# Own raw buffers for two weights of the output projection, and another order of temporaries in the first FFN product

## The chip, the cores and the metric

One core of a Trainium2 chip runs the whole program; the other cores are idle. The metric is the device time of one execution in microseconds (us), taken as the median of several runs. A profiled execution stands beside it, with a trace of every instruction. The engines are named as the profile names them: PE (matrix products, with PEld for its weight loads), DVE (vector engine), ACT (scalar engine), POOL (GpSimd) and SP (which here only issues transfers).

## The reference, cut to what matters

A decoder layer on 1024 tokens of width 1024: two attention branches are merged by gates, projected and added to the input; then a norm, a SwiGLU feed-forward net with inner width 2816, a second residual and a last norm.

```python
merged = (g_a * y_a + g_b * y_b).astype(x.dtype)
x = x + merged @ w_out[layer]                      # output projection

h2 = rms_norm(x, norm_ffn_g[layer])
gu = h2 @ w_ffn_in[layer]                          # first FFN product
x = x + (jax.nn.silu(gu[..., :D_FF]) * gu[..., D_FF:]) @ w_ffn_down[layer]
return rms_norm(x, norm_final_g)
```

Everything is float32.

## The kernel before, in words

**Splitting.** A float32 factor is split into a high part (a rounded copy by ACT, line 99) and a low part (the rest, by DVE, line 100); `split` does both. A product is then three matmuls: high by high, high by low, low by high (`mm3`, lines 104 to 106; `prod`, line 306). `load_w` asks for a raw weight on SP's queue (line 123), into a raw buffer with the tag `wr` (two buffers in `wpool`, unless it is given another pool as `rpool`), and splits it. A raw buffer is free again when DVE has made the low part. The parts lie in `w` tiles (two buffers in `wpool`) or, for tag `wo`, in two buffers of the stage's own pool. In the profile all raw buffers are named wr, all high parts wh and all low parts wl, after the names that the program gives its tiles.

**Output projection.** The stage runs twice over halves of 512 output columns (`c0` = 0 and 512), within each over two halves of 512 tokens (`hh`), within these over four groups `t` of 128 tokens; each group has a bank of PSUM and 24 matmuls, eight `k` of three. A weight tile covers two `k`, so each column half has four, `ws[0]` to `ws[3]`: the first two with their parts in `wpool`, the last two (k = 4 and 6) under `wo` in the stage's pool `mpool`. All four raw weights go through `wpool`'s two raw buffers. `pd()` hands out the banks from six in turn. `take(t)` adds a finished bank to the residual `x1` on DVE (line 1025). In the second column half the row of 128 tokens is then complete: `take` writes it out and calls `norm_transpose`, which squares it on ACT into a tile `hn` (line 174), works out the norm's factor on DVE, writes the normed row into `hn` (line 176), transposes it on PE in two groups of four (line 181) into a bank from a ring of two, splits the transposed values into `hT` and keeps an unsplit copy (line 187). `hn` has four buffers.

**Right sides.** Beside this, `right_side(n)` loads two blocks of the second FFN weight on SP (line 997), subtracts quarters from each other on POOL (line 1001) and writes the results out (line 1002), for eight `n`, with three buffers `r`; `sides(a, b)` does so for a range. They are used only in the last stage.

**First FFN product.** The first two of 22 column blocks are plain products (`plain(0)`, `plain(1)`, pool "first": a pad of 12 KB per partition and two buffers `a` of 4 KB). `plain(0)` starts with the first token half, placed around the last transposes (`behind`), and ends with the second. The others run as a block scheme of seven products instead of eight (`up`, pool "up"): `left_side` makes A1, S12, S34 and A22 out of raw weights, the sums on POOL (tile `s`), the parts by `split`; `c1`, `v2`, `v3`, `sg1` hold intermediate results and `a` the output. A1 is multiplied first, then S12. Pool "up" lies where pool "first" lay, so each of its tiles waits for what was in its place.

**Who orders the work.** Each engine takes its instructions strictly in a written order. That order is made at build time by a planner with cost estimates of its own; `tc.issue_after(i)` puts the instructions of a block behind `i` on the engine of `i`. `reserve` only claims places, in the order of its list, which fixes where each tile of the pool lies. The pool of the last stage, "down", lies in turn over hT, the block scheme's tiles and pool "up".

Of the kernel before, what the change touches and what calls it, by code (L numbers as in the profile page):

```python
# [8 lines left out]
F32 = mybir.dt.float32  # L9
F32R = mybir.dt.float32r  # L10
# [5 lines left out]
P = 128  # L16
D = 1024
S = 1024
KT = D // P
NT = S // P  # L20
HALF = 512
# [26 lines left out]
def layer_kernel(  # L48
# [59 lines left out]
    last_mm, last_hi, last_lo, last_sq = [None], [None], [None], [None]  # L108
# [104 lines left out]
    hT = [hT_all[:, :, hh * HALF:(hh + 1) * HALF] for hh in range(2)]  # L213
# [59 lines left out]
    def reserve(pool, *places):  # L273
        for tag, shape, dtype, bufs in places:
            for _ in range(bufs):
                pool.tile([P] + shape, dtype, tag=tag, name=nm(tag), bufs=bufs)
# [128 lines left out]
    with pool_of("foxv", 2) as vpool:  # L405
# [49 lines left out]
        for i in range(NT):  # L455
            load_x()
            hh, c = divmod(i * P, HALF)
# [115 lines left out]
    with pool_of("proj", 1) as upool:  # L573
# [3 lines left out]
        for pr in range(0, 4, 2):  # L577
            for a in range(2):
                c0 = FOX0 + a * FOX_W + pr * P
# [23 lines left out]
    fpool = f_ctx.__enter__()  # L603
# [305 lines left out]
    for i, (br, dt) in enumerate(merge_order):  # L909
        n = br * KT + dt  # L910
# [58 lines left out]
    TWO_ROWS = [(j, j + 1) for j in range(2, NFF - 4, 2)]  # L969
# [15 lines left out]
    blocks = [(f1[:], f3[:]), (f2, f4)]  # L985
# [4 lines left out]
    with pool_of("wout", 2) as mpool:  # L990
        gain2 = load_gain(mpool, norm_ffn_g)

        def right_side(n):

            r = mpool.tile([P, 2, 2, HALF], F32, tag="r", name=nm("r"), bufs=3)
            j = TWO_ROWS[n][0]
            last_w[0] = nc.sync.dma_start(out=r[:].rearrange("p n b c -> p n (b c)"),
                              in_=w_ffn_down[j * P:(j + 2) * P, :].rearrange("(n p) c -> p n c", p=P))
            b11, b12, b21, b22 = [r[:, i, b] for i in range(2) for b in range(2)]
            for out, p, q in ((b11, b12, b11), (b12, b22, b12), (b22, b22, b11), (b21, b22, b21)):  # L1000
                nc.gpsimd.tensor_tensor(out=out, in0=p, in1=q, op=ALU.subtract)
            nc.gpsimd.dma_start(out=rows_of(right_dram[n]), in_=r[:].rearrange("p n b c -> p (n b) c"))

        def sides(a, b):
            for n in range(a, b):
                with tc.issue_after(last_w[0].ins):
                    right_side(n)

        for c0 in range(0, D, HALF):
            ws = []  # L1010

            def load_out(k):
                src = w_out[k * P:(k + 2) * P, c0:c0 + HALF]
                ws.append(load_w(src, 2, HALF) if k < 4 else load_w(src, 2, HALF, tag="wo", pool=mpool))

            for hh in range(2):
                pts = [pd() for _ in range(4)]

                def mms(t, k):
                    mm3(pts[t][:], hT[hh][:, k, t * P:(t + 1) * P], ws[k // 2][:, k % 2], k == 0, k == KT - 1)  # L1020

                def take(t):
                    xt = x1[2 * hh + t // 2][:, t % 2]
                    xs = xt[:, c0:c0 + HALF]
                    nc.vector.tensor_tensor(out=xs, in0=pts[t][:], in1=xs, op=ALU.add)
                    if c0 > 0:
                        nc.scalar.dma_start(out=x1_dram[4 * hh + t], in_=xt)
                        norm_transpose(xt, gain2, hT[hh], t * P, mpool, True, 4, blocks[hh])

                if hh == 0 and c0 == 0:  # L1030
                    for k in range(KT):
                        if k % 2 == 0:
                            load_out(k)
                            if k < 6:
                                with tc.issue_after(last_w[0].ins):
                                    x_rows(k // 2)
                        for t in range(4):
                            mms(t, k)
                    sides(0, 3)
                    with tc.issue_after(last_w[0].ins):  # L1040
                        x_rows(3)
                    for t in range(4):
                        take(t)
                    continue
                if hh == 0:
                    for k in range(0, KT, 2):
                        load_out(k)
                        if k == 2:
                            sides(3, 5)
                    sides(5, len(TWO_ROWS))  # L1050
                for t in range(4):
                    for k in range(KT):
                        with tc.issue_after(last_mm[0].ins) if k == 0 else ExitStack():
                            mms(t, k)
                    take(t)


    a_dram = dpool.tile([NFF, P, S], F32, name="a_dram")
# [13 lines left out]
    with pool_of("first", 2) as fpool:  # L1072
# [48 lines left out]
        rpool = r_ctx.__enter__()  # L1121
# [1 line left out]
        split(T1.hi, T1.lo, f1[:])  # L1123

    with pool_of("up", 1) as fpool:
        reserve(fpool, ("s", [KT, P], F32, 2), *[("s34" + n, [KT, P], F32R, 1) for n in "hl"],
                *[("a22" + n, [4, P], F32R, 1) for n in "hl"],
                *[(n, [HALF], F32, 1) for n in ("c1", "v2", "v3", "sg1")], ("a", [S], F32, 2))

        def tmp(n):  # L1130
            return fpool.tile([P, HALF], F32, tag=n, name=nm(n), bufs=1)

        def up(j, todo, half):
            A1, S12, S34, A22 = left_side(fpool, *(odd if j == PLAIN + 1 else raws(j)), 2, 1)
            b1, b2, b3 = pd(), pd(), psf.tile([P, HALF], F32, tag="f", name=nm("pf"))
            a = fpool.tile([P, S], F32, tag="a", name=nm("a"), bufs=2)
            a1, a2 = a[:, :HALF], a[:, HALF:]
            c1, v2, v3, sg1 = [tmp(n) for n in ("c1", "v2", "v3", "sg1")]
            prod(b1, A1[:, :4], B11, True)
            with tc.issue_after(s12_hi[0].ins) if j == PLAIN else ExitStack():  # L1140
                nc.scalar.activation(out=c1[:], in_=b1[:], func=AF.Copy)
            prod(b2, S12[:, 4:], T2, True)
            vi = from_bank(v2[:], b2, c1)
            if todo:
                with tc.issue_after(vi.ins):
                    left_rows(*todo, 1)
            prod(b1, A1[:, 4:], B21)

            nc.scalar.activation(out=sg1[:], in_=b1[:], func=AF.Sigmoid)
            gi = from_bank(sg1[:], b1, sg1, ALU.mult)  # L1150
            if todo:
                with tc.issue_after(gi.ins):
                    left_rows(*todo, 2)
            prod(b2, S34[:, :4], T3)
            from_bank(v3[:], b2, c1)
            prod(b3, S12[:, :4], T1, True)
            ai = from_bank(a2, b3, v3)
            if half:
                with tc.issue_after(ai.ins):
                    left_rows(None, half, None, 0)  # L1160
            prod(b2, A22, T4)
            from_bank(a1, b2, c1)
            nc.gpsimd.tensor_tensor(out=a1, in0=a1, in1=sg1[:], op=ALU.mult)
            prod(b3, S34[:, 4:], B22)
            gt2, sg2 = tmp("v3"), tmp("sg1")
            from_bank(gt2[:], b3, v2)
            nc.scalar.activation(out=sg2[:], in_=gt2[:], func=AF.Sigmoid)
            nc.gpsimd.tensor_tensor(out=sg2[:], in0=gt2[:], in1=sg2[:], op=ALU.mult)
            nc.gpsimd.tensor_tensor(out=a2, in0=a2, in1=sg2[:], op=ALU.mult)
            return a[:].rearrange("p (b c) -> p b c", b=2)  # L1170

        def left_rows(n, p, q, part):

            if part == 0:
                ops = [(2, p[:, 0], p[:, 1], ALU.subtract)]
            elif part == 1:
                ops = [(0, p[:, 1], q[:, 1], ALU.add)]
            else:
                ops = [(1, f1[:, 0], p[:, 0], ALU.subtract), (3, q[:, 0], f1[:, 1], ALU.subtract)]
            for i, x_, y_, op in ops:  # L1180
                nc.vector.tensor_tensor(out=f1[:, i], in0=x_, in1=y_, op=op)
            if part == 2:
                nc.gpsimd.dma_start(out=rows_of(left_dram[n, 3:7]), in_=f1[:])

        todo, one = None, None
        for j in range(PLAIN, NFF):
            n, second = divmod(j - 2, 2)
            a = up(j, todo, one if second and n < len(TWO_ROWS) else None)
            todo = None
            if n >= len(TWO_ROWS):  # L1190
                nc.gpsimd.dma_start(out=a_dram[j], in_=a.rearrange("p b c -> p (b c)"))
            elif second:
                nc.gpsimd.dma_start(out=rows_of(left_dram[n, 1:3]), in_=a)
                todo = (n, one, a)
            else:
                nc.gpsimd.dma_start(out=left_dram[n, 0], in_=a[:, 0])
                one = a
# [187 lines left out]
```

## Time and profile before

| | |
|---|---|
| median of 3 runs | 1468.31 us (1468.17 to 1468.74) |
| the profiled execution | 1467.87 us |
| its span, first to last instruction | 1466.2 us |
| PE busy | 1439.0 us, 98% of the span |
| DVE, ACT, POOL busy | 945.9, 562.7, 493.0 us |
| mean granted clock of PE | 0.992 |

In the trace the first column half of the output projection ends at about 750.7 us, the second at about 806 us, the two plain products at about 853 us; the block scheme then runs to about 1243 us and the last stage to the end. How to read it: a row of a timeline gives start, duration, engine, line, operation, the tile written, the tiles read, the shapes and a count; in brackets stands how long the engine had been idle before, and what ended that. A row of waits gives the total, the number of waits and the longest. "ACTq" or "SPq" is an engine's queue of transfers to issue. PEclk is the clock that PE was granted, 1.00 at full speed. A busy PE is not a PE at full speed.

### The profile page before, as it was taken

What the parts mean: (1) busy time and instruction counts of PE and PEld (TensorE: products, weight loads), DVE (VectorE), ACT (ScalarE), POOL (GpSimd) and SP (SyncE); (2) the same over time, 40 slices, a digit from 0 to 9 for tenths busy, and PEclk for the clock granted to TensorE, in tenths of its full rate; (3) what the DMA queues carried; (4) which work ended last, traced back from release to release, by engine and by line L of the source; (5) the groups of instructions that cost most, each with busy time, mean ns of one, the idle gap of its engine ahead of it and who ended that gap; (6) DMA issues with size and microseconds to landing.
All of it is one profiled execution on the core that took longest, in us unless ns stands there. A gap on an engine that the chain in (4) does not pass through costs nothing.

```text
span 1466.2 us, 18397 instructions
## 1 busy us (share of the span) xinstructions
PE 1439.0 (98%) x6876; PEld 1165.2 (79%) x6876; DVE 945.9 (65%) x1332; ACT 562.7 (38%) x840; POOL 493.0 (34%) x438
## 2 busy tenths in 40 slices
PE   8999999999999999999989999999999999999997
PEld 7898888877777676788868878888888888888886
DVE  6484554359888999846626854566655655765655
ACT  5333332226656423354315522223322223644333
POOL 1021444535433321110074035566666664100000
PEclk9999999999999999999999999999999999999999
DMA  8232444575543561265796322233332332976512
GB/s 231 72 101 80 150 158 129 141 204 134 129 123 98 173 201 36 80 233 172 263 333 258 93 75 64 95 108 108 108 102 99 108 115 101 350 253 230 182 48 86
DMA packets 165785, 213.58 MB, mean 146 GB/s; under 512 B 13760, under 2 KB 115136, under 8 KB 165440
## 3 DMA queue, kind: packets, MB, share of 16 engines
q1 hardware_dynamic: 129376, 119.06, 25.8%
q0 software_dynamic: 15344, 55.59, 10.6%
q10 hardware_dynamic: 20976, 37.76, 8.2%
q8 instruction: 54, 0.88, 0.3%
q14 instruction: 35, 0.29, 0.1%
HBM read 146.32 MB, written 66.06 MB: 145 GB/s over the span
## 4 chain that ended last, share of the span: by engine, by line
PE 89%; DVE 6%; issue 1%; DMA 1%; ACT 1%; POOL 1%; SPq 1%; ACTq 0%; POOLq 0%; DVEq 0%
PE pd L306 30%; PE pd L1300 10%; PE pf L306 7%; PE pd L105 6%; PE pd L106 6%; PE pd L104 6%; PE pf L106 3%; PE pf L105 3%; PE pf L104 3%; PE pd L203 2%; PE pd L204 2%; PE pd L207 2%; PE pd L718 1%; PE pd L667 1%; PE pd L668 1%
## 5 line engine op out<-in xcount | busy, mean ns | idle before, releaser
L306 PE MATMUL pd<-tT,wh 128*128 128x512 f32 x768 | 235.5, 390 | 2.8 <-ACT wh L99 2.8
L100 DVE TENSOR_TENSOR wl<-wr,wh 128x1024 fp32r<-128x1024 f32 (+2 forms) x110 | 129.6, 1178 | 136.1 <-ACT wh L99 135.3
L99 ACT ACTIVATE wh<-wr 128x1024 fp32r<-128x1024 f32 (+2 forms) x110 | 95.4, 867 | 289.9 <-PE pd L306 163.0
L306 PEld LDWEIGHTS pd<-tT,wh 128*128 128x128 f32 x768 | 144.2, 188 | 33.2 <-ACT wh L99 3.2
L306 PE MATMUL pd<-hT_t,wh 128*128 128x512 f32 x536 | 167.0, 392 | 0.0
L306 PE MATMUL pd<-tT,wl 128*128 128x512 f32 x384 | 147.6, 389 | 0.0
L306 PEld LDWEIGHTS pd<-hT_t,wh 128*128 128x128 f32 x536 | 101.7, 190 | 21.6 <-ACT cc L332 0.2
L106 PE MATMUL pf<-hT_t,wl 128*128 128x512 f32 x288 | 114.1, 397 | 0.0
L104 PE MATMUL pf<-hT_t,wh 128*128 128x512 f32 x288 | 113.6, 395 | 0.0
L105 PE MATMUL pf<-hT_t,wh 128*128 128x512 f32 x288 | 113.2, 393 | 0.0
L292 POOL TENSOR_TENSOR s<-wr 128x512 f32<-128x512 f32 x29 | 53.3, 1839 | 157.9 <-DMA wr<-in_w_in_dram 72.9
L99 ACT ACTIVATE wh<-s 128x1024 fp32r<-128x1024 f32 x58 | 61.4, 1060 | 114.4 <-POOL s L293 87.3
L306 PE MATMUL pd<-hT_t,wl 128*128 128x512 f32 x268 | 105.0, 392 | 0.0
L99 ACT ACTIVATE oh<-raw 128x1024 fp32r<-128x1024 f32 x66 | 70.0, 1062 | 81.0 <-PE pd L1300 28.9
L306 PE MATMUL pf<-hT_t,wh 128*128 128x512 f32 x320 | 99.1, 391 | 0.0
L100 DVE TENSOR_TENSOR wl<-s,wh 128x1024 fp32r<-128x1024 f32 x58 | 71.7, 1238 | 33.9 <-ACT wh L99 33.9
L1300 PE MATMUL pd<-ol,oh 128*128 128x512 f32 x224 | 87.1, 389 | 0.0
L1300 PE MATMUL pd<-oh,ol 128*128 128x512 f32 x224 | 86.3, 389 | 0.0
L1300 PE MATMUL pd<-oh 128*128 128x512 f32 x224 | 84.7, 389 | 0.0
L104 PE MATMUL pd<-wh,hT_t 128*128 128x512 f32 (+1 forms) x208 | 77.7, 383 | 6.8 <-ACT wh L99 6.6
L306 PEld LDWEIGHTS pd<-tT,wl 128*128 128x128 f32 x384 | 72.1, 188 | 14.9
L105 PE MATMUL pd<-wl,hT_t 128*128 128x512 f32 (+1 forms) x208 | 80.0, 385 | 1.9 <-DVE wl L100 1.9
(287 smaller groups left out, 3234.1 us busy)
## 6 DMA issues: line engine op xcount, KB each, us to landing
wr<-in_w_in_dram SPq DMA_DIRECT2D x46, 512.0 KB, 4.6
wr<-in_w_ffn_in_dram SPq DMA_DIRECT2D x44, 512.0 KB, 3.8
raw<-left_dram SPq DMA_DIRECT2D x56, 256.0 KB, 5.3
g_dram<-fst ACTq DMA_DIRECT2D x32, 256.0 KB, 2.3
land<-g_dram SPq DMA_DIRECT2D x16, 512.0 KB, 3.5
r<-in_w_ffn_down_dram SPq DMA_DIRECT2D x8, 1024.0 KB, 8.5
right_dram<-r POOLq DMA_DIRECT2D x8, 1024.0 KB, 6.1
left_dram<-f POOLq DMA_DIRECT2D x8, 1024.0 KB, 4.9
```

Of the source, the lines that this page charges most:

```text
L99: last_hi[0] = nc.scalar.activation(out=hi, in_=src, func=AF.Copy)
L100: last_lo[0] = nc.vector.tensor_tensor(out=lo, in0=src, in1=hi.bitcast(F32), op=ALU.subtract)
L104: nc.tensor.matmul(psum, w.hi, m.hi, start=start, stop=False)
L105: nc.tensor.matmul(psum, w.hi, m.lo, start=False, stop=False)
L106: last_mm[0] = nc.tensor.matmul(psum, w.lo, m.hi, start=False, stop=stop)
L203: nc.tensor.matmul(pt[hh][:], w.hi[:, k], m.hi, start=(k == 0), stop=False)
L204: nc.tensor.matmul(pt[hh][:], w.hi[:, k], m.lo, start=False, stop=False)
L207: nc.tensor.matmul(pt[hh][:], w.lo[:, k], m.hi, start=False, stop=(k == kt - 1))
L292: nc.gpsimd.tensor_tensor(out=s12[:, :4], in0=u1, in1=u2, op=ALU.add)
L306: last_mm[0] = nc.tensor.matmul(bank[:], p, q, start=first and k == 0 and n == 0, stop=k == 3 and n == 2, skip_group_check=True)
L667: nc.tensor.matmul(pt[:, HALF - n:], kj, qx[e][:, qs], start=True, stop=False)
L1300: nc.tensor.matmul(bank[:], p, q, start=new and n == 0 and i == 0, stop=n == last and i == 2, skip_group_check=True)
```

## The change

In the second column half the weights k = 4 and 6 get raw buffers of their own in `mpool` (tag `wr`, two buffers of 4 KB per partition), and `hn` goes from four buffers to two, of 4 KB each. All four weights are asked for ahead of the right sides 3 to 7, where before right sides 3 and 4 stood between the second and the third. The last evacuation of the first column half (`take(3)` of the second token half) is set aside in `left` and written behind the low part of the fourth weight on DVE. In pool "up" the reserved order becomes s, c1, v2, a, s34, a22, v3, sg1; before it was s, s34, a22, c1, v2, v3, sg1, a. No matmul, split or transfer is added or removed.

```diff
+        left = []
         for c0 in range(0, D, HALF):
             ws = []
 
             def load_out(k):
                 src = w_out[k * P:(k + 2) * P, c0:c0 + HALF]
-                ws.append(load_w(src, 2, HALF) if k < 4 else load_w(src, 2, HALF, tag="wo", pool=mpool))
+                ws.append(load_w(src, 2, HALF) if k < 4 else
+                          load_w(src, 2, HALF, tag="wo", pool=mpool, rpool=mpool if c0 else None))
...
-                def take(t):
+                def take(t, hh=hh, pts=pts, c0=c0):
...
-                        norm_transpose(xt, gain2, hT[hh], t * P, mpool, True, 4, blocks[hh])
+                        norm_transpose(xt, gain2, hT[hh], t * P, mpool, True, 2, blocks[hh])
...
                 if hh == 0:
                     for k in range(0, KT, 2):
                         load_out(k)
-                        if k == 2:
-                            sides(3, 5)
-                    sides(5, len(TWO_ROWS))
+                    sides(3, len(TWO_ROWS))
+                    with tc.issue_after(last_lo[0].ins):
+                        left[0](3)
                 for t in range(4):
                     for k in range(KT):
                         with tc.issue_after(last_mm[0].ins) if k == 0 else ExitStack():
                             mms(t, k)
-                    take(t)
+                    if c0 == 0 and t == 3:
+                        left.append(take)
+                    else:
+                        take(t)
...
-        reserve(fpool, ("s", [KT, P], F32, 2), *[("s34" + n, [KT, P], F32R, 1) for n in "hl"],
-                *[("a22" + n, [4, P], F32R, 1) for n in "hl"],
-                *[(n, [HALF], F32, 1) for n in ("c1", "v2", "v3", "sg1")], ("a", [S], F32, 2))
+        reserve(fpool, ("s", [KT, P], F32, 2), *[(n, [HALF], F32, 1) for n in ("c1", "v2")], ("a", [S], F32, 2),
+                *[("s34" + n, [KT, P], F32R, 1) for n in "hl"], *[("a22" + n, [4, P], F32R, 1) for n in "hl"],
+                *[(n, [HALF], F32, 1) for n in ("v3", "sg1")])
```

## The prediction

> **What bounds the kernel now.** The page first: which engine fills the span, and who ends the chain.
>
> ```profile
> span 1466.2 us, 18397 instructions
> PE   1439.0 (98%) x6876; PEld 1165.2 (79%) x6876; DVE 945.9 (65%) x1332; ACT 562.7 (38%) x840; POOL 493.0 (34%) x438
> PE 89%; DVE 6%; issue 1%; DMA 1%; ACT 1%; POOL 1%; SPq 1%; ACTq 0%; POOLq 0%; DVEq 0%
> ```
>
> TensorE is the bound nearly everywhere, and the change touches none of its matmuls. It can only save idle PE time and slow PE time, so the waits of PE come next, longest first.
>
> ```profile
> PE pd L104 <- ACT wh L99: 6.6, 2, 4.5
> PE pd L306 <- ACT wh L99: 2.8, 1, 2.8
> ```
>
> The two largest single waits (4.5 and 2.8 us) lie inside the two stages that the diff edits. The windows around them show the clock beside the wait (first number: length; then PE busy and records; PEclk after POOL):
>
> ```profile
> 750.72:753.44 2.72, 2.72 (x13) 2.06 (x11) 0.69 (x1) 0.00 (x0) 2.56 (x3) 1.00 1.03 388
> 753.44:758.10 4.66, 0.16 (x1) 0.00 (x0) 0.02 (x1) 1.06 (x1) 3.03 (x3) 0.75 1.04 400
> 758.10:762.79 4.69, 4.22 (x10) 2.99 (x10) 2.43 (x2) 1.06 (x1) 1.80 (x2) 0.52 1.02 417
> 815.50:821.00 5.50, 5.50 (x28) 4.65 (x29) 3.69 (x5) 4.05 (x6) 0.00 (x0) 1.00 0.00 0
> 855.93:858.87 2.94, 0.16 (x2) 0.00 (x1) 0.71 (x2) 1.63 (x3) 0.00 (x0) 0.88 0.23 92
> 858.87:865.24 6.37, 6.37 (x16) 4.98 (x17) 6.13 (x4) 3.38 (x4) 3.79 (x3) 0.52 0.61 168
> 865.24:870.00 4.76, 4.76 (x22) 3.94 (x21) 3.72 (x4) 1.54 (x2) 4.68 (x3) 1.00 0.00 0
> ```
>
> A count includes the matmul under way at the edge: 13 records in 2.72 us are 12 steps of 0.227 us. Stall one costs 4.66 us, then 9 steps take 4.69 us at a clock of 0.52, where 9 x 0.227 = 2.04 would do: 2.65 more. Stall two costs 2.94 us, then 15 steps take 6.37 us instead of 3.40: 2.97 more. So **7.31 us** hang on the first stall and **5.91 us** on the second. Behind 865 us no wait of PE is listed up to the end, so what is saved here should arrive at the end whole.
>
> **Stall one, the late weights.** The first row is from the chain of waits and names the transfer; the others, picked from the timelines of SP, ACT and DVE, say why it was late.
>
> ```profile
> 749.23 7.66 DMA wr<-in_w_out_dram
> 722.18 3.98 SPq L123 DMA_DIRECT2D wr<-in_w_out_dram  x2
> 749.23 1.73 SPq L123 DMA_DIRECT2D wr<-in_w_out_dram  x2
> 746.89 1.06 ACT L99 ACTIVATE wh<-wr 128x1024 fp32r<-128x1024 f32 x1 [28.15 <-PE pd L106]
> 748.25 1.06 ACT L99 ACTIVATE wh<-wr 128x1024 fp32r<-128x1024 f32 x1 [0.30 <-PE pd L106]
> 757.00 1.06 ACT L99 ACTIVATE wh<-wr 128x1024 fp32r<-128x1024 f32 x1 [7.69 <-DMA wr<-in_w_out_dram]
> 758.33 1.06 ACT L99 ACTIVATE wh<-wr 128x1024 fp32r<-128x1024 f32 x1 [0.27 <-DMA wr<-in_w_out_dram]
> 747.98 2.58 DVE L100 TENSOR_TENSOR wl<-wr,wh 128x1024 fp32r<-128x1024 f32 x2 [1.81 <-ACT wh L99]
> ```
>
> Raw weights k=0, 2 are asked for at 722; k=4, 6 need the same two buffers, which are freed only when DVE has split the first two, from 749.2 on. With own buffers, k=4, 6 go out directly behind k=2, near 726, and have 23 us for a transfer that took 7.66 beside full DMA. The splits are then bound by PE alone, which must finish with the old ws[2] and ws[3] (tag wo, two buffers). The old half's last group starts at 745.28 (six steps of 0.227 a pair): ws[2] is free at 749.4, ws[3] at 750.7. High parts at 749.6 and 751.0 (1.06 us each); low parts on DVE follow. These now meet POOL, whose subtractions of the right side run then:
>
> ```profile
> 750.19 5.58 POOL L1001 TENSOR_TENSOR r<-r 128x512 f32<-128x512 f32 x4 [2.53 <-DMA r<-in_w_ffn_down_dram]
> 860.21 1.28 POOL L292 TENSOR_TENSOR s<-wr 128x512 f32<-128x512 f32 x1 [13.23 <-issue]
> 858.85 1.23 DVE L100 TENSOR_TENSOR wl<-s,wh 128x1024 fp32r<-128x1024 f32 x1 [0.26 <-ACT wh L99]
> 860.27 2.30 DVE L100 TENSOR_TENSOR wl<-wr,wh 128x1024 fp32r<-128x1024 f32 x1 [0.20 <-ACT wh L99]
> ```
>
> The same split takes 1.23 us alone and 2.30 beside POOL. I take 2.30: low ws[2] 750.7 to 753.0, low ws[3] 753.0 to 755.3. PE reaches k=4 at 753.44 and k=6 at 754.80, and wants the low part one step later (753.67, 755.03). The first is there, the second 0.3 us late. Bounds: 0 if POOL is not in the way, 0.6 if ws[2] is hit too. Taken: **0.3**.
>
> What else moves here. The right sides 3 and 4 were asked for ahead of k=4; now they stand behind it on SP. They wait for a write of POOL anyway, and the two transfers ahead of them wait for nothing: 0, and later sides lose the competition at 749 to 757. The old half's last evacuation goes behind the fourth low split on DVE:
>
> ```profile
> 750.92 0.69 DVE L1025 TENSOR_TENSOR x<-pd,x 128x512 f32<-128x512 f32 x1 [0.35 <-PE pd L106]
> ```
>
> It moves to about 755.3, done by 756.0; next on DVE is the evacuation of the new half's first group, ready near 756.5. Its bank is one of six and comes back six groups later. Cost 0; if it slipped into that evacuation, 0.69 us of DVE, with no PE wait.
>
> **hn from four buffers to two.** This pays for the space. The Square of token tile t then waits for the second group of transposes of t-2. In the rows, Squares of tiles 5, 6, 7 against the last transposes of tiles 3, 4, 5 (0.60 us long):
>
> ```profile
> 796.38 1.05 ACT L174 ACTIVATE hn<-x 128x1024 f32<-128x1024 f32 x1
> 801.11 1.06 ACT L174 ACTIVATE hn<-x 128x1024 f32<-128x1024 f32 x1 [1.26 <-DVE r L165]
> 809.14 1.05 ACT L174 ACTIVATE hn<-x 128x1024 f32<-128x1024 f32 x1
> 796.86 0.60 PE L181 MATMUL pt<-ident,hn 128*128 128x128 f32 x4
> 803.92 0.60 PE L181 MATMUL pt<-ident,hn 128*128 128x128 f32 x4
> 810.77 0.60 PE L181 MATMUL pt<-ident,hn 128*128 128x128 f32 x4
> ```
>
> They would start 1.1, 3.4 and 2.2 us later (with the 1.1 inherited from tile 5, 3.3 for tile 7). Behind a waiting Square stand the hT copies of earlier tiles on ACT, and so PE's transposes. The cover is the first FFN product's half that needs only tiles 0 to 3; the second half starts at 820.57 and needs tile 7's last low part 12 steps (2.7 us) later:
>
> ```profile
> 820.40 0.68 DVE L100 TENSOR_TENSOR hT_t<-pt,hT_t 128x512 fp32r<-128x512 f32 x1
> 820.57 0.61 PE L104 MATMUL pd<-hT_t,wh 128*128 128x512 f32 x2
> ```
>
> Ready at 821.1, wanted at 823.3: 2.2 us of slack against some 3.4 late. Bounds 0 and 1.2, more if PE's order itself changes; taken **0.5**. A stall that short need not slow the clock: after 0.47 us at 815.50 it stayed 1.00.
>
> **Stall two, the order of the temporaries.** First a row of the chain, then rows of ACT, POOL and DVE.
>
> ```profile
> 854.50 2.64 DMA a_dram<-a
> 847.96 1.92 ACT L99 ACTIVATE hT_t<-f 128x2048 fp32r<-128x2048 f32 x1 [3.82 <-PE pd L207]
> 857.24 0.63 ACT L99 ACTIVATE wh<-wr 128x512 fp32r<-128x512 f32 x1 [7.36 <-DMA a_dram<-a]
> 857.77 1.04 ACT L99 ACTIVATE wh<-s 128x1024 fp32r<-128x1024 f32 x1
> 845.69 1.29 POOL L298 TENSOR_TENSOR s<-wr,s 128x512 f32<-128x512 f32 x1
> 853.18 1.29 DVE L1087 TENSOR_TENSOR a<-pd,a 128x512 f32<-128x512 f32 x2 [0.97 <-PE pd L207]
> ```
>
> Sizes per partition: the earlier pool is a 12 KB pad, then two a of 4 KB. Over it lay s 8, s34 high 4 (the pad's end), s34 low 4 (first a), a22 high and low 4 (second a). So a22's copy on ACT waits until the second a is written out, and S12's copy, whose source POOL finished by 847.0, queues behind it; PE stands for S12. Reordered: s 8, c1 and v2 4 fill the pad, the new a lies on the old a (first written after the bank joins, far past 857), and s34, a22, v3, sg1 lie beyond. Then ACT is free from 849.9: both copies by 851.6, before PE is there at 855.93. On DVE the worst order is both evacuations (to 854.5), low a22 (0.7), low S12 (1.23): 856.4, just when PE's second step wants it. Bounds 0 and 1.2 (low s34 ahead as well); taken **0.3**.
>
> The same order moves the last stage's tiles: its raw rows lie on v3, sg1 instead of on a (this wait goes), and one xf lies on the last a.
>
> ```profile
> SPq L1285 <- DMA a_dram<-a: 18.2, 1, 18.2
> ```
>
> PE has no wait there either way; xf is wanted only in the second product. 0.
>
> **The sum,** against the profiled execution (1467.87 us, its span 1466.2 and 1.67 around it; 0.44 under the median 1468.31): 1467.87 - 7.31 + 0.3 + 0.5 - 5.91 + 0.3 = 1455.75. With the 0.44 that the median lies higher: **1456.2**. With no leftovers, 1455.1.
>
> **Rivals.**
> (a) hn binds more than I charge. Tile 5 takes 15.0 us from its Square (796.38) to the end of its last transposes (811.37). If that length stays, two buffers let one tile through each 7.5 us; PE's own pace is 24 steps, 5.44 us, and two groups of transposes at some 0.4 each beside their overlap, 6.2 together. 1.3 us x 5 tiles = 6.5 late, less 2.2 of slack, 4.3 at most, 2 at half of it: 1458 to 1460. For it: ACT takes its work strictly in its order. Against it: most of the 15 us is waiting for a place in PE's queue, not work.
> (b) One stall only goes. If S12's copy keeps a late place for another reason (a planner sets the order): 1456.2 + 5.6 = 1461.8. If the raw weights are still late: 1456.2 + 7.0 = 1463.2. Against both: the rows name the releasers, and the change removes exactly these.
> (c) The slow stretch from 858.87 is not the second stall's. Then 2.97 stays: 1459.2. Against it: the clock is 1.00 before and 0.52 directly after, as after stall one. The Trainium skill, "TensorE: Matmul & The Clock Gate", Part 1, has the clock fall to half only after an idle window of about 3.4 us, free-running; by that rule 2.94 us of idleness need not have caused it, and the time would be this rival's. The trace disagrees, 0.52 after 2.94 us.
> (d) Slower: hn's two buffers lengthen the chain itself, since PE's transposes wait for copies behind a Square that waits for transposes. To eat 12.2 us and 2.2 of slack over five tiles, each tile must lose 2.9 us, a chain of 2 x (6.2 + 2.9) = 18.2 us. At 22 us: 5 x 4.8 = 24, less 14.4, about 10 slower, 1478. Tile 5's 15.0 is the longest chain of the rows above, and no Square waited for hn before.
> (e) Nothing moves: the loads near 726 are held by space of the stage before, and ACT's order stays. 1468.
>
> **Chances.** Forecast (1455 to 1458) 0.62; (a) 0.13; (b) 0.12; (c) 0.04; (d) 0.05; (e) 0.04. Range 1454.0 to 1462.0: forecast, (a), (c) and half of (b). About 0.2% (2.9 us) is what a measurement can tell here. Faster 0.91, same 0.04, slower 0.05.
>
> **What would show it.** PE's 4.5 us wait at L104 and the 2.8 at L306 gone from the list, four w_out loads in one SP row near 722 to 728, clock 1.00 through both places, no ACT wait on a_dram<-a. Wrong: a Square waiting for PE's transposes for microseconds and a new PE wait at L181 or in the first product's second half; or A22's or S12's copy still behind something at 855.

## The result and the profile after

The changed kernel takes **1458.40 us** (median of 5 runs, 1457.72 to 1459.35) against 1468.31 (5 runs, 1467.40 to 1468.74): a ratio of 0.9934, 95% interval 0.9920 to 0.9949. That is 9.9 us faster where 12.1 were forecast, and 2.2 us over the forecast of 1456.2. The profiled execution took 1458.40 us as well. The page's span, busy times and chain, to be set beside those of before:

```profile
span 1456.7 us, 18390 instructions
PE 1436.4 (99%) x6876; PEld 1165.2 (80%) x6876; DVE 944.9 (65%) x1332; ACT 562.4 (39%) x840; POOL 495.2 (34%) x438
PE 91%; DVE 6%; issue 1%; ACT 1%; DMA 1%; POOL 1%; SPq 0%; ACTq 0%; POOLq 0%; DVEq 0%
```

PE is 2.6 us less busy with the same 6876 records: it ran less at the low clock. The list of PE's waits from 690 us to the end (total, times, longest) is now one row:

```profile
PE pt L181 <- DVE hn L176: 2.7, 1, 2.7
```

Both stalls of before are gone and a new one has come, where the prediction said that a wrong step would show: at L181, the transposes of the norm. PE's own rows give the size of each piece. The matmul that opens the first FFN product, the first one of the block scheme, the one at which the slow stretch of stall two is over, and the last one of all, before:

```profile
806.20 0.39 PE L104 MATMUL pd<-hT_t,wh 128*128 128x512 f32 x1
853.21 0.61 PE L306 MATMUL pd<-hT_t,wh 128*128 128x512 f32 x2
870.00 0.61 PE L306 MATMUL pd<-hT_t,wh 128*128 128x512 f32 x2
1457.30 0.39 PE L106 MATMUL pd<-oh,ol 128*128 128x512 f32 x1
```

The same four after, and with them the opening of that product's second half (817.27; 820.57 before):

```profile
799.06 0.39 PE L104 MATMUL pd<-hT_t,wh 128*128 128x512 f32 x1
817.27 0.62 PE L104 MATMUL pd<-hT_t,wh 128*128 128x512 f32 x2
849.91 0.62 PE L306 MATMUL pd<-hT_t,wh 128*128 128x512 f32 x2
860.88 0.61 PE L306 MATMUL pd<-hT_t,wh 128*128 128x512 f32 x2
1448.17 0.39 PE L106 MATMUL pd<-oh,ol 128*128 128x512 f32 x1
```

The lead is 7.14 us behind the output projection, 3.30 at the second half (3.84 given back in between), 3.30 at 849.91, 9.12 behind stall two (5.82 gained), 9.13 at the last matmul. So stall one, hn and stall two measured 7.14, 3.84 and 5.82 us, where the prediction had 7.31 - 0.3, 0.5 and 5.91 - 0.3. The last 0.4 us of the span lie in the closing transfers.

The two cured places, in the table by windows (length, PE busy, and so on; PEclk after POOL):

```profile
750.92:753.64 2.72, 2.72 (x14) 2.25 (x13) 2.58 (x3) 1.06 (x1) 0.45 (x1) 1.00 1.02 399
753.64:758.00 4.36, 4.36 (x21) 3.62 (x20) 1.09 (x2) 0.35 (x1) 4.12 (x4) 1.00 1.11 347
807.49:810.63 3.14, 0.40 (x3) 0.03 (x1) 2.70 (x7) 1.41 (x3) 0.00 (x0) 1.00 0.00 0
810.63:814.46 3.83, 3.83 (x14) 3.26 (x15) 1.38 (x2) 2.89 (x4) 0.00 (x0) 0.57 0.00 0
852.63:860.88 8.25, 8.25 (x38) 6.68 (x37) 6.70 (x5) 4.99 (x6) 6.60 (x4) 1.00 0.62 162
```

Rows 1, 2 and 5: PE never idle, clock 1.00. Rows 3 and 4 are the new place: PE idle for nearly 3 us, then the clock at 0.57. How the cures came about, first on SP and POOL, then ACT, then DVE (picked rows of their timelines):

```profile
722.27 8.31 SPq L123 DMA_DIRECT2D wr<-in_w_out_dram  x4
753.19 5.49 POOL L1001 TENSOR_TENSOR r<-r 128x512 f32<-128x512 f32 x4 [5.88 <-DMA r<-in_w_ffn_down_dram]
```

```profile
751.12 1.06 ACT L99 ACTIVATE wh<-wr 128x1024 fp32r<-128x1024 f32 x1 [0.30 <-PE pd L106]
...
846.49 0.61 ACT L99 ACTIVATE wh<-wr 128x512 fp32r<-128x512 f32 x1
847.01 1.04 ACT L99 ACTIVATE wh<-s 128x1024 fp32r<-128x1024 f32 x1
```

```profile
748.18 5.26 DVE L100 TENSOR_TENSOR wl<-wr,wh 128x1024 fp32r<-128x1024 f32 x4 [1.81 <-ACT wh L99]
...
851.69 1.22 DVE L100 TENSOR_TENSOR wl<-s,wh 128x1024 fp32r<-128x1024 f32 x1
```

All four weights go out in one row of SP; the fourth high part is made at 751.12, when PE lets go of its place, not at 758.33 when its data came. Four low parts take 5.26 us, some 1.3 each: POOL was not in the way until the last of them was nearly done, since the data of its right side came at 753.19 and not, as before, at 750.19. At stall two the copies of A22 and S12 stand at 846.49 and 847.01, directly behind the copy before them, instead of 857.24 and 857.77.

**The new wait.** Rows of ACT, DVE and PE around it, in this order:

```profile
804.27 0.59 ACT L99 ACTIVATE hT_t<-pt 128x512 fp32r<-128x512 f32 x1
804.75 1.06 ACT L174 ACTIVATE hn<-x 128x1024 f32<-128x1024 f32 x1
```

```profile
809.20 1.28 DVE L176 SCALAR_TENSOR_TENSOR hn<-x,r,gain 128x1024 f32<-128x1024 f32 x1
```

```profile
803.62 0.60 PE L181 MATMUL pt<-ident,hn 128*128 128x128 f32 x4
807.49 0.40 PE L106 MATMUL pd<-hT_t,wl 128*128 128x512 f32 x1
810.63 1.48 PE L181 MATMUL pt<-ident,hn 128*128 128x128 f32 x8 [2.74 <-DVE hn L176]
817.04 0.39 PE L106 MATMUL pd<-hT_t,wl 128*128 128x512 f32 x1
```

Tile 7's Square (804.75) has to wait for tile 5's last transposes (803.62, until 804.22), and then for tile 5's copy in front of it on ACT. Before it stood at 809.14, which less the 7.14 gained is 802.00: it is 2.75 us late. Its square root and its normed row (809.20 to 810.48) follow, and PE, which had run out of matmuls at 807.72 (the start of the last one, 807.49, and a step of 0.227), takes tile 7's transposes at 810.63. Eighteen matmuls of the first half (811.76 to 817.04) need nothing of tile 7, but they stand behind these transposes in PE's written order. At the same place before:

```profile
814.63 0.40 PE L106 MATMUL pd<-hT_t,wl 128*128 128x512 f32 x1
815.50 0.66 PE L181 MATMUL pt<-ident,hn 128*128 128x128 f32 x4 [0.47 <-ACT x L187]
```

PE was idle there for 0.64 us already (814.86 to 815.50, counted in the same way), waiting for a bank. Now it is 2.91, 2.27 more. Behind it the first 3.83 us at a clock of 0.57 lost 1.66 us, against 0.05 before. 2.27 + 1.61 = 3.88, the 3.84 given back.

### The profile page after: what moved, and what is told of

Read it like the earlier page. It is cut to its first block, busy times and chain, and to the rows that moved or that the text cites. A ratio compares the mean times of both kernels' runs of the same rounds, so it can differ in the third digit from the quotient of the medians.

```text
span 1456.7 us, 18390 instructions
## 1 busy us (share of the span) xinstructions
PE 1436.4 (99%) x6876; PEld 1165.2 (80%) x6876; DVE 944.9 (65%) x1332; ACT 562.4 (39%) x840; POOL 495.2 (34%) x438
## 4 chain that ended last, share of the span: by engine, by line
PE 91%; DVE 6%; issue 1%; ACT 1%; DMA 1%; POOL 1%; SPq 0%; ACTq 0%; POOLq 0%; DVEq 0%
PE pd L306 30%; PE pd L1305 10%; PE pf L306 7%; PE pd L105 7%; PE pd L104 7%; PE pd L106 7%; PE pf L106 3%; PE pf L105 3%; PE pf L104 3%; PE pd L203 2%; PE pd L204 2%; PE pd L207 2%; PE pd L718 1%; PE pd L667 1%; PE pd L668 1%
## 5 line engine op out<-in xcount | busy, mean ns | idle before, releaser
L105 PE MATMUL pf<-hT_t,wh 128*128 128x512 f32 x288 | 113.4, 394 | 0.0
L105 PE MATMUL pd<-wl,hT_t 128*128 128x512 f32 (+1 forms) x208 | 79.8, 384 | 0.8 <-DVE wl L100 0.8
L100 DVE TENSOR_TENSOR ol<-raw,oh 128x1024 fp32r<-128x1024 f32 x66 | 76.2, 1219 | 6.6 <-ACT oh L99 6.6
```

The source lines that it names most:

```text
L100: last_lo[0] = nc.vector.tensor_tensor(out=lo, in0=src, in1=hi.bitcast(F32), op=ALU.subtract)
L105: nc.tensor.matmul(psum, w.hi, m.lo, start=False, stop=False)
```

## The experiments

Twelve kernels (their diffs are shortened here), in three groups, each group with runs of the kernel before on its own chip: 1468.38 (15 runs, 1464.61 to 1469.95), 1467.72 (15 runs, 1464.82 to 1469.55) and 1467.68 (9 runs, 1466.41 to 1470.37).

| kernel | us, median | lowest to highest | ratio to before, 95% |
|---|---|---|---|
| e1: before, new order in "up" | 1461.64 | 1461.55 to 1463.29 | 0.9963 (0.9951 to 0.9976) |
| e2: after, old order in "up" | 1463.78 | 1461.87 to 1465.47 | 0.9972 (0.9962 to 0.9982) |
| e3: after, hn of four tiles in raw buffers | 1454.98 | 1454.80 to 1456.12 | 0.9916 (0.9902 to 0.9929) |
| e4: before, two hn | 1471.06 | 1468.67 to 1472.68 | 1.0023 (1.0013 to 1.0034) |
| e5: after, right sides 3 and 4 in between | 1457.84 | 1457.71 to 1459.35 | 0.9936 (0.9922 to 0.9950) |
| e6: after, shared raw buffers | 1462.23 | 1460.74 to 1463.51 | 0.9964 (0.9951 to 0.9976) |
| e7: after, evacuation in place | 1459.50 | 1457.77 to 1460.02 | 0.9942 (0.9930 to 0.9955) |
| e8: before, stall two filled | 1465.98 | 1464.14 to 1467.34 | 0.9987 (0.9978 to 0.9996) |
| e9: after, once more | 1459.38 | 1456.34 to 1459.51 | 0.9932 (0.9918 to 0.9945) |
| e10: e3, once more | 1454.83 | 1454.55 to 1455.92 | 0.9911 (0.9898 to 0.9925) |
| e11: after, three hn | 1454.58 | 1454.29 to 1456.13 | 0.9910 (0.9897 to 0.9924) |
| e12: after, tile 7's wait filled | 1456.63 | 1456.21 to 1457.03 | 0.9922 (0.9909 to 0.9936) |

**e1 and e2: the two parts apart.** e1 is the kernel before with the new `reserve`; e2 the changed kernel with the old one.

```diff
-        reserve(fpool, ("s", [KT, P], F32, 2), s34 h/l, a22 h/l, c1, v2, v3, sg1, ("a", [S], F32, 2))
+        reserve(fpool, ("s", [KT, P], F32, 2), c1, v2, ("a", [S], F32, 2), s34 h/l, a22 h/l, v3, sg1)
```

> The kernel before with the new order of pool "up" alone. Theory A (the second stall is a22's and S12's copies behind the write of the old a, and the slow stretch after it is its consequence): 2.94 + 2.97 = 5.9 us less, about 1462.5 us; no wait of ACT on a_dram, clock 1.00 behind it. Rival (the slow stretch has another cause): 2.9 less, 1465.4.

> The changed kernel with the old order of pool "up": the output projection's edits alone. Theory A (7.3 us of the first stall go, hn's two buffers give back 3.8 at tile 7's transposes): about 3.5 less than before, 1464.9 us, the 2.8 us wait at L306 back and the new wait at L181 still there. Rival (the two edits are not additive, the new wait at L181 comes from both together): 7.3 less, 1461.0, no long wait at L181.

Measured: e1 6.7 us under before, e2 4.6 under before. PE's waits in e1, then in e2:

```profile
PE pd L104 <- ACT wh L99: 4.0, 1, 4.0
PE pt L181 <- ACT x L187: 0.5, 1, 0.5
```

```profile
PE pd L306 <- ACT wh L99: 2.8, 1, 2.8
PE pt L181 <- DVE hn L176: 2.8, 1, 2.8
```

Each part takes away its own stall and leaves the other, and the new wait at L181 comes with the projection's part alone. The two gains, 6.7 and 4.6, add up to 11.3 where both together gave 9.9; the difference is well within the spread of the kernels that still have a stall (3.6 us from lowest to highest in e2, 5.3 in the kernel before).

**e3, e4, and e10, e11 with the changed kernel e9 beside them: is it hn?** e3 (and e10, the same) puts the `hn` of tiles 2, 3, 6 and 7 into `mpool`'s two raw buffers, idle by then; e4 is the kernel before with `hn` cut to two; e11 has three, for which there is room.

```diff
 e3, e10: hn = pool.tile([P, D], F32, tag="hn", ..., bufs=2)
       +  if t > 1: hn = pool.tile([P, 2, HALF], F32, tag="wr", ..., bufs=2)
 e4:   -  norm_transpose(xt, gain2, hT[hh], t * P, mpool, True, 4, blocks[hh])
       +  norm_transpose(xt, gain2, hT[hh], t * P, mpool, True, 2, blocks[hh])
 e11:  -  norm_transpose(xt, gain2, hT[hh], t * P, mpool, True, 2, blocks[hh])
       +  norm_transpose(xt, gain2, hT[hh], t * P, mpool, True, 3, blocks[hh])
```

> The changed kernel, with the norm tiles of token tiles 2, 3, 6, 7 in the two new raw weight buffers, which are idle by then: four hn places again in the same space. Theory A (two hn buffers hold tile 7's Square): the wait of 2.74 us at L181 and the slow stretch behind it go, 3.8 less than the changed kernel, 1454.6 us. Rival B (tile 7 is late because the stage starts 7 us earlier and ACT, DVE and POOL are packed tighter; hn is not it): 1458.4, the wait stays.

> The kernel before with hn at two buffers and nothing else. Theory A: both old stalls stay and tile 7's transposes stand for hn as in the changed kernel: 3.8 more, 1472.1 us, with a wait of some 2.7 us at L181. Rival B (the earlier start is what makes tile 7 late): 1468.3, no such wait.

> The changed kernel unaltered, for a comparison on one chip with the next three. Both theories: 1458.4, between 1457.7 and 1459.4 as in its earlier runs, with the 2.7 us wait of PE at L181.

> The changed kernel with the hn of tiles 2, 3, 6 and 7 in the raw buffers that have gone idle. Theory A (hn's two buffers give back the 3.4 to 3.8 us): 1455.0, 3.4 under the changed kernel on the same chip. Rival B (the 3.4 between the two was a difference of chips): 1458.4.

> The changed kernel with three buffers of hn instead of two, nothing else. Theory A (only the Square of tile 7, which waits for the transposes of tile 5, is late by 2.75 us; with three buffers it waits for tile 4's, which are some 7 us earlier): no wait of PE at L181 over 0.5 us, 1455.0. Rival B (one more buffer only shifts the wait to a later place, or the raw buffers freed PE in another way): 1456.5 to 1458.4.

e4 is 2.7 us slower than the kernel before. Its list has the new wait beside the two old ones:

```profile
PE pd L104 <- ACT wh L99: 4.9, 1, 4.9
PE pd L306 <- ACT wh L99: 2.8, 1, 2.8
PE pt L181 <- DVE hn L176: 2.7, 1, 2.7
```

So two buffers make the wait without any other part of the change. With e3, e10 and e11 it goes, and so does what was given back: on one chip 1454.83 and 1454.58 against e9's 1459.38; none of their eight runs lies above 1456.13, none of e9's below 1456.34. Of the 5.3 us between the profiled executions of e9 and e11 at the last matmul, 3.85 lie at tile 7; the other 1.5 had come before 745 us, in stages that are the same in both. The wait that is left in e11, its Square and its transposes of tile 7:

```profile
PE pt L181 <- ACT x L187: 0.5, 1, 0.5
```

```profile
801.51 1.05 ACT L174 ACTIVATE hn<-x 128x1024 f32<-128x1024 f32 x1
```

```profile
807.86 0.66 PE L181 MATMUL pt<-ident,hn 128*128 128x128 f32 x4 [0.47 <-ACT x L187]
```

The Square stands 3.2 us earlier than after (804.75) and PE waits only for the bank, as before. **e11 is the version that beats both kernels:** one number more, 1454.58 us, 0.9910 of before.

**e5, e6, e7: which piece of the projection's part cures stall one.** e5 puts right sides 3 and 4 back between the second and third weight and keeps the own buffers; e6 keeps the order and takes the own buffers away; e7 writes the last evacuation in its old place.

```diff
 e5:    load_out(k)
     +  if k == 2: sides(3, 5)
     -  sides(3, len(TWO_ROWS))
     +  sides(5, len(TWO_ROWS))
 e6: -  rpool=mpool if c0 else None
     +  rpool=None
 e7: -  with tc.issue_after(last_lo[0].ins): left[0](3)
     -  if c0 == 0 and t == 3: left.append(take)
     -  else: take(t)
     +  take(t)
```

> The changed kernel with right sides 3 and 4 asked for between k=2 and k=4 again, as before; own raw buffers kept. Theory A (the own buffers do it; the planner puts transfers that wait for nothing ahead of those that wait for POOL whatever the text says): 1458.4 us, the four loads still in one SP row near 722. Rival (asking first does it): k=4 and 6 behind right side 3, from 745 or later, a stall of some us before 758: about 1464 us.

> The changed kernel without own raw buffers: all four weights asked for first, but through the two shared buffers. Theory A (the buffers do it): k=4 and 6 wait for DVE's first low parts, the first stall is back with its slow stretch, 7.3 more than the changed kernel: 1465.7 us. Rival (asking first is enough): 1458.4.

> The changed kernel with the last evacuation of the first column half in its old place, ahead of DVE's third low part instead of behind the fourth. Theory A (there is slack on DVE, the set-aside does nothing): 1458.4 us within 0.5, no wait of PE near 753. Rival (DVE is tight there): the third and fourth low parts are 0.7 late, a wait of up to 0.7 us near 754, 1459.1.

e5 equals the changed kernel: the planner puts the four weights first on SP by itself, now that they wait for nothing (four in one row from 721.95, the next right side at 744.60). e6 is 4.4 us slower than e5 on the same chip; SP's row, then PE's waits:

```profile
722.15 28.84 SPq L123 DMA_DIRECT2D wr<-in_w_out_dram  x4
```

```profile
PE pd L104 <- ACT wh L99: 2.7, 1, 2.7
PE pt L181 <- DVE hn L176: 1.1, 1, 1.1
```

The four requests last 28.84 us instead of 8.31, since the third waits for DVE. Stall one is back, if shorter than before (2.7 against 4.5). The two late weights are asked for when they were before, at 749.25 and 750.62, but the first copy of their data stands at 755.20 instead of 757.00; right side 3, asked for ahead of them at 744.00 before, now comes behind them (751.09). So the own buffers are the cure; the order of asking seems to matter only where they are missing. That e6 lost less than the 7.3 expected has its main reason in the list: tile 7's wait fell to 1.1, which gives some 3 of the 3.84 us back. Why it fell was not followed up. e7 has no PE wait near 754 us, and from 745 us to the last matmul its profiled execution gained 9.3 us on before, just as the changed kernel's did; the 1.8 us that it lost on before lie in the stages ahead of that. Setting the evacuation aside did nothing that shows.

**e8 and e12: is the slow clock the stall's?** e8 is the kernel before with 12 matmuls of ones in stall two, into a bank that is overwritten later; e12 the changed kernel with 9 in front of tile 7's transposes. The waits stay; only PE is not idle in them.

```diff
 e8:  after prod(b1, ...), first block only:
   +  for _ in range(12): nc.tensor.matmul(b3[:, :P], ones[:], ones[:], start=True, stop=True)
 e12: in norm_transpose, tile 7, first group:
   +  for _ in range(9): nc.tensor.matmul(pt[:, :P], ones[:], ones[:], start=True, stop=True)
```

> The kernel before with 12 small matmuls of ones (128 x 128 columns, into a bank that is cleared afterwards) behind A1's first product of the first block, so that PE is busy in most of the 2.94 us in which it stands for S12; S12's copy comes as late as before. Theory A (the idle time sets the clock back): the slow stretch behind it goes, 3.0 less, 1465.3 us, clock near 1.00 behind 859. Rival (the slow stretch has another cause, or 2.9 us of idleness do not matter): 1468.3, clock 0.52 behind 859.

> The changed kernel with 9 matmuls of ones (18 passes of about 0.12 us, 2.1 us) in front of tile 7's transposes, into the bank that these then overwrite. The wait itself stays, only its idleness goes. Theory A (the clock falls behind the idle 2.9 us and costs 1.66 of the 3.84 given back): clock 1.00 behind the transposes, 1456.8. Rival B (the clock falls there for another reason, or costs nothing over several runs): 1458.4.

The fills on PE, in e8 and in e12 (whose added lines put the fill at L181):

```profile
857.73 2.84 PE L1143 MATMUL pf<-ones 128*128 128x128 f32 x24
```

```profile
807.83 2.27 PE L181 MATMUL pt<-ones 128*128 128x128 f32 x18 [0.48 <-ACT x L189]
```

In e8's windows the clock stays 1.00 behind the fill, with 26 records in 6.00 us:

```profile
860.74:866.74 6.00, 6.00 (x26) 4.98 (x27) 5.74 (x4) 3.43 (x5) 3.44 (x2) 1.00 0.63 176
```

e8 is 1.7 us faster than before, though PE does more work. e12 comes to 1456.63, as expected (1456.8), 2.1 above e11: that is the wait alone. So the idleness brings the slow clock, and useless matmuls in its place avoided it in both profiles.

At stall two alone e8's profiled execution gained 2.76 of the 2.97: its lag of 1.81 us on before, 1.15 of it from stages ahead of 745 us that e8 leaves as they are, became a lead of 0.95.

But idleness doesn't bring the slow clock each time. The same stall two of 2.94 us, with PE busy 0.15 or 0.16 us of it, stands in e2 and in e4; the 6.00 us behind it in e2, then in e4:

```profile
853.85:859.85 6.00, 6.00 (x20) 4.86 (x21) 5.75 (x4) 3.43 (x5) 3.45 (x2) 0.72 0.65 179
```

```profile
862.50:868.50 6.00, 6.00 (x26) 4.99 (x27) 5.75 (x3) 3.42 (x5) 3.46 (x2) 1.00 0.65 179
```

20 records at 0.72 and 26 at 1.00, where the profile of before had the clock at 0.52 for 6.37 us. The loss was 2.98 us in before, 1.69 in e2 and 0.14 in e4. After tile 7's wait, also 2.9 us idle, it was 1.66 in the changed kernel, 0.05 in e2 and 1.31 in e4. Stall one, 4 us and more in before, e1, e4 and e8, lost 2.5 to 3.1 us with the second wait of 0.5 us (L105) that follows it; e6's shorter one of 2.7, with 0.6 behind it, lost 3.9. Tile 7's shorter waits, up to 1.3 us idle (e6), lost under 0.1.

Windows cut where the clock itself changes show more; stall two in before, then in e2, then in e4:

```profile
855.93:858.16 2.23, 0.16 (x1) 0.00 (x0) 0.26 (x1) 0.92 (x2) 0.00 (x0) 1.00 0.30 121
858.16:864.99 6.83, 6.12 (x14) 4.79 (x15) 6.34 (x5) 4.09 (x5) 3.54 (x3) 0.50 0.57 157
850.37:853.78 3.41, 0.70 (x4) 0.24 (x2) 0.69 (x1) 1.56 (x3) 0.00 (x0) 1.00 0.35 144
853.78:857.19 3.41, 3.34 (x8) 2.69 (x9) 3.15 (x2) 2.40 (x4) 1.92 (x2) 0.50 0.67 195
858.13:861.55 3.42, 1.58 (x7) 0.97 (x6) 0.01 (x1) 0.68 (x2) 0.00 (x0) 1.00 0.38 153
861.55:864.96 3.41, 2.46 (x11) 2.04 (x12) 2.95 (x3) 3.28 (x4) 1.12 (x1) 1.00 0.37 108
```

In all fourteen traces the granted clock is either 1.00 or 0.50, a slow stretch up to the last matmul lasts 3.41 or 6.83 us, and two of one trace start a whole number of 3.413 us apart (in before 755.76 and 858.16: 30 of them). A step of 3.41 us at half clock costs 1.7 us when PE is busy throughout. So 1.69 in e2 is one step, 2.98 in before is two, and e6's short stall lost more than the long one of before because its slow stretch (756.49 to 763.31) lay almost wholly behind it, while 2.3 us of the other (755.76 to 762.59) fell into the stall itself. How a gap lies on this grid fits its price: in the seven gaps of 2.9 us that brought the slow clock (before, the changed kernel, one each in e2 and e4, e5, e7, e9), one step had PE busy for 1.40 us or less; in the two that did not, the gap was shared by two steps (1.58 and 2.46 us busy at stall two in e4; 1.78 and 2.30 at tile 7 in e2). No run moved a gap along the grid to test this, and it is no threshold for every stage: in the changed kernel the clock also fell at 551.72 us, behind a step with 2.11 us busy.

e9's five runs, 1456.34 and 1456.74 against 1459.38 to 1459.51, differ by more than one step. The profiled one (1459.38) lost 1.66 us behind tile 7's wait, and has another slow stretch of 6.83 us at 569.87, in a stage that the change leaves alone; what the two faster runs were spared is not recorded.

## Why the prediction was right, and where not

- **Stall one** was right in its place, its cause and its size: 7.14 us measured against 7.01. The own buffers are the cause (e6 against e5), as the prediction read it from the rows of SP. The 0.3 us for low parts beside POOL did not come; the step took POOL's rows of before as they stood, though the change itself moved them.
- **Stall two** was right: 5.82 against 5.61. The 0.3 for DVE's worst order did not come either. The new order of pool "up" alone takes the stall away (e1); that A22's copy behind the write of a was the mechanism is what the rows name, and no run moved that tile alone.
- **hn** is the step that failed: "Ready at 821.1, wanted at 823.3: 2.2 us of slack against some 3.4 late", and the 0.5 taken from it. The term measured 3.84 in the profiled execution: 2.27 for the wait, the rest for the clock behind it. The lateness was near enough (2.75 of 3.3), but the slack was read where the results are used, in the second half. PE meets tile 7 earlier, at its transposes, 18 matmuls before; there it was waiting already (0.47 at 815.50), and the slack of hn's chain was 2.75 - 2.27 = 0.48 us. The first half was the cover only for what stands behind it in the written order, not for what stands in front.
- **"A stall that short need not slow the clock"** was argued from one of 0.47 us and used for one of 2.9. In the changed kernel it did, for 1.6 us (e12 takes it away), while in e2 the same wait cost 0.05.
- **Rival (a)**, hn binding more, is what happened, at its price of 1458 to 1460 (the forecast itself was 1455 to 1458), though not by its working: not five tiles each 1.3 us late, but one tile at one place. e4 and e11 show it.
- **Rival (b)** fell: both stalls went (the list of waits). **(d)** and **(e)** fell with the result.
- **Rival (c)**, that the slow stretch is not the stall's, fell in e8: with the gap filled the clock stayed. Yet 2.97 us is one execution's price, not the stall's fixed one. The Trainium skill, "TensorE: Matmul & The Clock Gate", Part 1, has the clock fall after at least one idle window of about 3.4 us that runs freely, so that the outcome varies with its phase. The runs agree on the free-running step (3.413 us) and that the outcome varies (2.98, 1.69 and 0.14 us behind the same 2.94), but not that a whole window must be idle: the clock fell behind gaps shorter than that window.

The sum: 1455.75 for the profiled execution, less 0.13 (stall one), plus 3.34 (hn), less 0.21 (stall two), less 0.37 (the closing transfers) is 1458.38; it took 1458.40. The range held it. How near it comes is owed in part to the clock of that one execution: behind tile 7's wait alone the runs show 0.05 to 1.66 us.

## What to carry to other kernels

When a buffer count is cut, follow the late instruction to the first place where the bounding engine's written order needs it, and measure the slack there; work that is independent, but written behind that place, covers nothing. Buffers for a weight's raw data are worth their space when the requests behind them would wait for a split; the order of asking then matters little. A wait of the tensor engine should be priced with the clock behind it, as a range (here none, one or two steps of some 1.7 us) and not as the value of one profile.

## What had not been expected of the hardware

Idle gaps of PE of equal length cost very different amounts: behind 2.9 us the granted clock fell to half for 6.83 us (2.98 us lost), for 3.41 (1.3 to 1.7) or not at all (0.05 to 0.14). The spread from run to run does not follow from such gaps alone: it is 3.6 us in e2, 4.0 in e4 and 3.2 in e9, but 1.6 in the changed kernel and in e5, against 1.3 to 1.8 in e3, e10 and e11, which have none, and 0.8 in e12, whose gap is filled. Twelve matmuls of ones, 2.84 us of useless work on PE, went with a time 0.9987 (0.9978 to 0.9996) of the kernel before's; the profiled execution shows the gain at stall two.
